# An output projection in seven half-size products, and both closing stages put into the list schedule

## The chip, the cores and the metric

The kernel runs on one core of one Trainium2 chip. The metric is the device time of one execution in microseconds (us), lower is better. The engines are TensorE (PE, matmuls into the accumulator memory PSUM), VectorE (DVE), ScalarE (ACT), GpSimd (POOL) and SyncE (SP, whose queue issues most DMA transfers).

## What is computed

One layer of an encoder for 1280 tokens of width D = 1024: a prompt of 1024 and a sample of 256 tokens, each with its own `gate` row. After a large input projection come a convolution branch and a bidirectional mLSTM branch. Cut to what matters here:

```python
g_conv, g_mlstm = jnp.split(jax.nn.sigmoid(gmerge), 2, axis=-1)
merged = g_conv * (y_conv @ w_proj_conv) + g_mlstm * (y_m @ w_proj_mlstm)
return x + gate * (merged @ w_out)            # then rms_norm(x, final_norm_g)
```

All three weight matrices here are 1024 x 1024, in float32.

## The kernel before

Every float32 product is made of three matmuls: each operand is split into a high part (a cast on ACT to the matmul's type) and a low part (the rest, a subtraction on DVE or POOL), and high x high, high x low and low x high are added up in PSUM. The input projection, up to about 1160 us, already multiplies by Strassen's scheme. The mLSTM stage and the convolution branch's projection follow until 1437 us. They are issued by a list scheduler, `Board`: each operation is recorded with its engine, an assumed duration, what it reads and writes and a step, and `board.play()` works out an order for each engine and issues the instructions in it. The two stages of this case come last. They are written by hand, in program order, behind that `play()`, and the framework adds the semaphores that their tiles need.

The tokens are worked on in two halves of 640 (five tiles of 128), the second half first. For each half:

- `merge` (L1799 and L1802 in the trace) calls `proj_y`, the product of y_m with w_proj_mlstm. The result has channels on the partitions: eight blocks of 128 channels, each with two accumulators of 320 tokens (q = 0, 1). For each accumulator PE runs 8 x 3 matmuls with 320 columns (L1596 to L1598). The weights are loaded in pairs of blocks (`raw`), and split by ACT (L275) and POOL (L276). `th` (the gate's part) and `zc` (the convolution branch's part, already multiplied) come from DRAM, through SP. DVE reads the accumulator in `times_1p` (L617), adds `zc` (L1799) and makes the low part `mL` (L1802); ACT makes the high part `mH`.
- `finish` is the output projection and the closing norm. Each half of w_out's columns is loaded and split by ACT (L1880) and DVE (L1881). For each of five token tiles and each half of the columns, `product_o` runs 8 x 3 matmuls with 512 columns (L1818 to L1820). In `residual`, DVE multiplies the accumulator by the gate (L1825) and adds it to `ob`, which holds x (L1826); ACT sums the squares (L1827), POOL multiplies by the final norm's weights (L1829). `norm_out` (from L1849) takes the root (ACT L1851), improves it with four small DVE instructions, scales the tile and sends it out. The very last column half of tile 4 is worked in two pieces of 256 columns (`last_part`, L1835 to L1840), and its scaling is shared by ACT (L1864) and DVE (L1865).

Every accumulator is a PSUM tile of its own, one bank with 512 floats in each partition. Eight of them are taken in turn:

```python
psD = [ctx.enter_context(tc.tile_pool(name=f"psD{n}", bufs=n, space=PSUM)) for n in (2, 6)]
def acc_d():
    taken[0] += 1
    return psD[(taken[0] - 1) % 8 < 6].tile([P, 512], F32, tag="acc", name="accd")
```

So PE can write one accumulator while DVE reads another, and it needs one again only eight accumulators later.

Of the kernel before, what the change touches and what calls it, by code (L numbers as in the profile page):

```python
# [9 lines left out]
F32 = mybir.dt.float32  # L10
# [171 lines left out]
def encoder_kernel(  # L182
# [40 lines left out]
    p1_dr = dram.tile([2, P, TH2], F32, name="p1_dr")  # L223

# [69 lines left out]
    hp = ctx.enter_context(tc.tile_pool(name="hp", bufs=1, side="right"))  # L294
# [1043 lines left out]
    thp = ctx.enter_context(tc.tile_pool(name="thp", bufs=3, side="right"))  # L1338
# [245 lines left out]
    def proj_y(src, y, acc_of, made=None):  # L1584

        for n2 in range(0, KT, 2):
            raws = made[0] if made and n2 == 0 else load_pair(wp, src, n2 * P, (n2 + 1) * P, 3)
            for nb in range(2):
                ws = made[1] if made and n2 + nb == 0 else [split_w(wp, r[:, :, nb * P:(nb + 1) * P], G) for r in raws]
                accs = [acc_of() for _ in range(2)]  # L1590
                for q in range(2):
                    qs = slice(q * TQ, (q + 1) * TQ)
                    for kt in range(KT):
                        wh, wl = (w[:, kt % 4, :] for w in ws[kt // 4])
                        yH, yL = (t[:, kt % 4, qs] for t in y[kt // 4])
                        PE.matmul(accs[q][:, :TQ], wh, yH, start=kt == 0, stop=False)  # L1596
                        PE.matmul(accs[q][:, :TQ], wh, yL, start=False, stop=False)  # L1597
                        PE.matmul(accs[q][:, :TQ], wl, yH, start=False, stop=kt == KT - 1)  # L1598
                    yield n2 + nb, q, accs[q]

# [153 lines left out]
    ym0.append(first_ym(1))  # L1754
    board.play()
    ym0 = [[[b.t for b in y] for y in ym0]]
    made_m = [b.t for b in raws_m], [[b.t for b in w] for w in ws_m]
    hand.close()
    mstack.close()
    bstack.close()  # L1760
    yr = ctx.enter_context(tc.tile_pool(name="yr", bufs=1, side="right"))

    def load_y(src, t0):
        v = src[:].rearrange("(k p) t -> p k t", p=P)
        res = []
        for n in range(2):
            yH, yL = (yq.tile([P, 4, TH2], F32R, tag=f"y{2 * n + part}", name="y") for part in range(2))
            for k in range(0, 4, 2):
                raw = yr.tile([P, 2, TH2], F32, tag="yraw", name="yraw")
                dma(raw[:], v[:, 4 * n + k:4 * n + k + 2, t0:t0 + TH2])  # L1770
                A.copy(yH[:, k:k + 2], raw[:])
                V.tensor_tensor(out=yL[:, k:k + 2], in0=raw[:], in1=fp(yH[:, k:k + 2]), op=ALU.subtract)
            res.append((yH, yL))
        return res

    psD = [ctx.enter_context(tc.tile_pool(name=f"psD{n}", bufs=n, space=PSUM)) for n in (2, 6)]
    taken = [0]
    wo_p = ctx.enter_context(tc.tile_pool(name="wo", bufs=2))  # L1780
    ep = ctx.enter_context(tc.tile_pool(name="ep", bufs=2))
    mgp = ctx.enter_context(tc.tile_pool(name="mgp", bufs=1))
    gbc = [mgp.tile([P, D], F32, name=f"gbc{s}") for s in range(2)]
    fng = mgp.tile([P, D], F32, name="fng")

    def acc_d():
        taken[0] += 1
        return psD[(taken[0] - 1) % 8 < 6].tile([P, 512], F32, tag="acc", name="accd")

    def merge(t0, y, mH, mL, made=None):  # L1790
        for n, q, acc in proj_y(wpm, y, acc_d, made):
            if q == 0:
                th = thp.tile([P, TH2], F32, tag="th", bufs=3, name="th")
                zc = ep.tile([P, TH2], F32, tag="zc", name="zc")
                dma(th[:], th_dr[D + n * P:D + (n + 1) * P, t0:t0 + TH2])
                dma(zc[:], zc_dr[n * P:(n + 1) * P, t0:t0 + TH2])
            qs = slice(q * TQ, (q + 1) * TQ)
            times_1p(th[:, qs], th[:, qs], acc[:, :TQ])
            V.tensor_tensor(out=th[:, qs], in0=th[:, qs], in1=zc[:, qs], op=ALU.add)  # L1799
            mh, ml = (m[n // 4][:, n % 4, qs] for m in (mH, mL))  # L1800
            A.copy(mh, th[:, qs])
            V.tensor_tensor(out=ml, in0=th[:, qs], in1=fp(mh), op=ALU.subtract)  # L1802

    def finish(c0, last, mH, mL):

        n5 = range(TH2 // P)
        ob = mgp.tile([P, 5, D], F32, tag="ob", name="ob")
        ssq = ep.tile([P, 5, 3], F32, tag="ssq", name="ssq")
        ms = ep.tile([P, 5], F32, tag="ms", name="ms")
        for j in n5:  # L1810
            dma(ob[:, j, :], x_rows(c0 + j))

        def product_o(pd, half, ws, j, cs=slice(0, 512)):
            ts_ = slice(j * P, (j + 1) * P)
            for k in range(4):
                kt = 4 * half + k
                sH, sL = mH[half][:, k, ts_], mL[half][:, k, ts_]
                PE.matmul(pd, sH, ws[0][:, k, cs], start=kt == 0, stop=False)  # L1818
                PE.matmul(pd, sH, ws[1][:, k, cs], start=False, stop=False)  # L1819
                PE.matmul(pd, sL, ws[0][:, k, cs], start=False, stop=kt == KT - 1)  # L1820

        def residual(pd, j, n2):
            ns = slice(n2 * 512, (n2 + 1) * 512)
            t = ep.tile([P, 4 * P], F32, tag="t", name="t")
            V.tensor_tensor(out=t[:], in0=pd, in1=gbc[0 if c0 + j < 8 else 1][:, ns], op=ALU.mult)  # L1825
            V.tensor_tensor(out=ob[:, j, ns], in0=ob[:, j, ns], in1=t[:], op=ALU.add)  # L1826
            A.activation(t[:], ob[:, j, ns], AF.Square, bias=zero[:, 0:1], scale=1.0,  # L1827
                         accum_out=ssq[:, j, n2:n2 + 1])
            G.tensor_tensor(out=ob[:, j, ns], in0=ob[:, j, ns], in1=fng[:, ns], op=ALU.mult)  # L1829

        def last_part(pd, i):

            ns = slice(512 + 256 * i, 768 + 256 * i)
            t = ep.tile([P, 4 * P], F32, tag="t", name="t")[:, 0:256]
            V.tensor_tensor(out=t, in0=pd[:, 0:256], in1=gbc[0][:, ns], op=ALU.mult)  # L1835
            V.tensor_tensor(out=ob[:, 4, ns], in0=ob[:, 4, ns], in1=t, op=ALU.add)
            V.tensor_tensor_reduce(out=t, in0=ob[:, 4, ns], in1=ob[:, 4, ns], op0=ALU.mult, op1=ALU.add, scale=1.0,
                                   scalar=0.0, accum_out=ssq[:, 4, 1 + i:2 + i])
            if i == 0:
                V.scalar_tensor_tensor(out=ms[:, 4:5], in0=ssq[:, 4, 1:2], scalar=1.0 / D, in1=ms[:, 4:5], op0=ALU.mult,  # L1840
                                       op1=ALU.add)

        def part_sums():
            V.tensor_scalar(out=ms[:], in0=ssq[:, :, 0], scalar1=1.0 / D, scalar2=EPS, op0=ALU.mult, op1=ALU.add)

        def norm_out(j0, j1):
            n, js = j1 - j0, slice(j0, j1)
            v, r, t = ms[:, js], *(ep.tile([P, n], F32, tag=f"n{i}", name=f"n{i}")[:] for i in range(2))
            V.scalar_tensor_tensor(out=v, in0=ssq[:, js, 2 if last and j0 == 4 else 1], scalar=1.0 / D, in1=v, op0=ALU.mult,  # L1849
                                   op1=ALU.add)  # L1850
            A.activation(r, v, AF.Sqrt, bias=zero[:, 0:1], scale=1.0)  # L1851
            V.reciprocal(r, r)
            if n == 1:
                V.scalar_tensor_tensor(out=t, in0=r, scalar=r, in1=v, op0=ALU.mult, op1=ALU.mult)
            else:
                V.tensor_tensor(out=t, in0=r, in1=r, op=ALU.mult)
                V.tensor_tensor(out=t, in0=t, in1=v, op=ALU.mult)
            V.tensor_scalar(out=t, in0=t, scalar1=-0.5, scalar2=1.5, op0=ALU.mult, op1=ALU.add)
            V.tensor_tensor(out=r, in0=t, in1=r, op=ALU.mult)
            for j in range(j0, j1):  # L1860
                rj = r[:, j - j0:j - j0 + 1]
                if last and j == 4:
                    hs = slice(0, D // 2), slice(D // 2, D)
                    A.activation(ob[:, j, hs[0]], ob[:, j, hs[0]], AF.Copy, bias=0.0, scale=rj)  # L1864
                    V.scalar_tensor_tensor(out=ob[:, j, hs[1]], in0=ob[:, j, hs[1]], scalar=rj, in1=fng[:, hs[1]],  # L1865
# [7 lines left out]
        def weights_o(n2, half):  # L1873
# [8 lines left out]
            return wh, wl  # L1882

        for n2 in range(2):
            ws = [weights_o(n2, half) for half in range(2)]
            if last and n2 == 1:

                for j in range(4):
# [64 lines left out]
```

## Time and profile before

| what | value |
|---|---|
| runs of the kernel | 1671.61, 1673.78, 1674.88 us |
| median | 1673.78 us |
| profiled execution | 1672.24 us |
| its span in the trace | 1670.5 us |
| mean granted clock of PE | 0.992 |
| first matmul of the merge | at 1437.19 us |
| first matmul of the last output projection | at 1605.22 us |

The page gives each engine's busy time as a share of the span, and follows back the chain of work that ended last. Rows of groups give the busy time and the mean duration of one instruction, and behind the last bar the idle time ahead of them with what ended it. Rows of the timeline give the start and the duration in us. Consecutive matmuls overlap, so the distance of their starts, not their duration, is what one costs.

### The profile page before, as it was taken

What the parts mean: (1) busy time and instruction counts of PE and PEld (TensorE: products, weight loads), DVE (VectorE), ACT (ScalarE), POOL (GpSimd) and SP (SyncE); (2) the same over time, 40 slices, a digit from 0 to 9 for tenths busy, and PEclk for the clock granted to TensorE, in tenths of its full rate; (3) what the DMA queues carried; (4) which work ended last, traced back from release to release, by engine and by line L of the source; (5) the groups of instructions that cost most, each with busy time, mean ns of one, the idle gap of its engine ahead of it and who ended that gap; (6) DMA issues with size and microseconds to landing.
All of it is one profiled execution on the core that took longest, in us unless ns stands there. A gap on an engine that the chain in (4) does not pass through costs nothing.

```text
span 1670.5 us, 27720 instructions
## 1 busy us (share of the span) xinstructions
PE 1634.5 (98%) x10552; PEld 1566.6 (94%) x10552; DVE 993.8 (59%) x1698; ACT 573.4 (34%) x1113; POOL 677.1 (41%) x498
## 2 busy tenths in 40 slices
PE   6999999999999999999999999999999999999997
PEld 3989999999999999999999999999888898998986
DVE  4885334556555566556656886652157777555645
ACT  4643332134453222222222211121256665333322
POOL 2243333335564666677666643333210001323412
PEclk8999999999999999999999999999999999999999
DMA  9434335324553122221222555458888855773631
GB/s 361 127 97 142 102 106 117 79 71 125 144 156 104 51 70 70 83 82 59 59 75 71 142 132 143 124 132 256 284 250 274 274 188 176 254 265 108 242 109 64
DMA packets 284697, 240.83 MB, mean 144 GB/s; under 512 B 96164, under 2 KB 239764, under 8 KB 284564
## 3 DMA queue, kind: packets, MB, share of 16 engines
q1 hardware_dynamic: 284388, 238.78, 46.7%
q8 instruction: 84, 1.38, 0.3%
q14 instruction: 49, 0.40, 0.1%
q10 hardware_dynamic: 176, 0.27, 0.0%
HBM read 170.12 MB, written 68.89 MB: 143 GB/s over the span
## 4 chain that ended last, share of the span: by engine, by line
PE 94%; DVE 2%; DMA 2%; SPq 1%; ACT 1%; issue 0%; POOL 0%; DVEq 0%; ACTq 0%
PE acc L807 64%; PE u L1441 3%; PE qc L1401 3%; PE accd L1597 2%; PE accd L1596 2%; PE accd L1598 2%; PE accd L1820 2%; PE accd L1818 2%; PE accd L1819 2%; PE acc L1665 2%; PE acc L1666 2%; PE acc L1667 2%; PE misc L1524 1%; PE misc L1484 1%; PE misc L436 1%; DMA raw<-in_w_in_dram 1%
## 5 line engine op out<-in xcount | busy, mean ns | idle before, releaser
L318 POOL TENSOR_TENSOR wl<-comb,wh 128x512 fp32r<-128x512 f32 x176 | 248.9, 1415 | 289.9 <-ACT wh L317 279.0
L716 DVE TENSOR_TENSOR q<-acc,q 128x640 f32<-128x640 f32 x272 | 220.8, 819 | 222.1 <-PE acc L807 216.8
L318 POOL TENSOR_TENSOR wl<-raw,wh 128x512 fp32r<-128x512 f32 x138 | 191.6, 1389 | 232.2 <-ACT wh L317 220.2
L807 PE MATMUL acc<-xt,wh 128*128 128x320 f32 x1408 | 264.0, 309 | 0.0
L807 PEld LDWEIGHTS acc<-xt,wh 128*128 128x128 f32 x1408 | 220.8, 188 | 0.2
L317 ACT CAST wh<-comb 128x512 fp32r<-128x512 f32 x176 | 108.8, 619 | 298.0 <-PE acc L807 261.3
L317 ACT CAST wh<-raw 128x512 fp32r<-128x512 f32 x138 | 85.3, 619 | 273.4 <-PE acc L807 204.1
L807 PE MATMUL acc<-xt,wl 128*128 128x320 f32 x704 | 160.5, 309 | 0.0
L1624 POOL TENSOR_TENSOR wl<-raw,wh 128x512 fp32r<-128x512 f32 x28 | 36.5, 1309 | 222.9 <-ACT wh L1623 222.4
L807 PEld LDWEIGHTS acc<-xt,wl 128*128 128x128 f32 x704 | 117.7, 188 | 0.0
L672 DVE TENSOR_TENSOR comb<-raw 128x512 f32<-128x512 f32 x88 | 71.4, 811 | 44.6 <-DMA raw<-in_w_in_dram 32.4
L875 POOL TENSOR_TENSOR big<-big,q 128x640 f32<-128x640 f32 x48 | 78.6, 1638 | 37.1 <-DVE q L716 28.7
L614 ACT ACTIVATE q<-q,zero 128x640 f32<-128x640 f32 x76 | 63.0, 831 | 82.6 <-DVE q L716 78.4
L672 DVE TENSOR_TENSOR comb<-raw,comb 128x512 f32<-128x512 f32 x44 | 46.7, 1061 | 63.3 <-POOL wl L318 63.2
L807 PE MATMUL acc<-t3L,wh 128*128 128x320 f32 x352 | 81.5, 313 | 2.7 <-DVE t3L L369 2.7
L807 PE MATMUL acc<-t3H,wh 128*128 128x320 f32 x352 | 81.3, 313 | 1.4 <-ACT t3H L368 1.4
L807 PE MATMUL acc<-b00H,wh 128*128 128x320 f32 x352 | 82.5, 316 | 0.0
L807 PE MATMUL acc<-b10H,wh 128*128 128x320 f32 x352 | 80.7, 311 | 0.8 <-ACT q L730 0.8
L807 PE MATMUL acc<-t3H,wl 128*128 128x320 f32 x352 | 81.4, 313 | 0.0
L807 PE MATMUL acc<-b11H,wh 128*128 128x320 f32 x352 | 81.3, 312 | 0.0
L807 PE MATMUL acc<-b00L,wh 128*128 128x320 f32 x352 | 80.8, 311 | 0.0
L807 PE MATMUL acc<-b00H,wl 128*128 128x320 f32 x352 | 80.5, 310 | 0.0
(322 smaller groups left out, 4116.4 us busy)
## 6 DMA issues: line engine op xcount, KB each, us to landing
raw<-in_w_in_dram SPq DMA_DIRECT2D x120, 256.0 KB
raw<-in_w_in_dram SPq DMA_DIRECT2D x34, 512.0 KB
th<-th_dr SPq DMA_DIRECT2D x31, 320.0 KB
th_dr<-q SPq DMA_DIRECT2D x28, 320.0 KB
raw<-in_w_proj_conv_dram SPq DMA_DIRECT2D x16, 512.0 KB
raw<-in_w_proj_mlstm_dram SPq DMA_DIRECT2D x16, 512.0 KB
raw<-in_w_out_dram SPq DMA_DIRECT2D x16, 512.0 KB
k<-kn_dr SPq DMA_DIRECT2D x56, 128.0 KB
```

Source lines behind the costliest of these rows:

```text
L317: op("ACT", .63, lambda: A.copy(wh[:], src()), r=r, w=[wh])
L318: op("POOL", 1.4, lambda: G.tensor_tensor(out=wl[:], in0=src(), in1=fp(wh[:]), op=ALU.subtract), r=[*r, wh], w=[wl])
L614: A.activation(out, in_, AF.Tanh, bias=zero[:, 0:1], scale=0.5)
L672: op("DVE", .9, lambda: V.tensor_tensor(out=t[:], in0=x(), in1=y(), op=o), r=[x.tok, y.tok], w=[t])
L716: op("DVE", .82, lambda: V.tensor_tensor(out=two(dst()), in0=acc[:, :, 0:TQ], in1=two(t()), op=ALU.add), r=[acc, t.tok], w=[dst.tok])
L807: PE.matmul(acc[:, q, 0:TQ], st_[:, k_, :], m_[:, q * TQ:(q + 1) * TQ], start=k_ == 0 and n == 0, stop=k_ == 3 and n == 2)
L875: op("POOL", 1.65, lambda: G.tensor_tensor(out=dst(), in0=dst(), in1=t(), op=ALU.mult), r=[dst.tok, t.tok], w=[dst.tok])
L1401: PE.matmul(pq[:, 0:HD + 2], qTs[i][:, kd, c * P:(c + 1) * P], C[:, kd, :], start=kd == 0, stop=kd == 1)
L1441: PE.matmul(pu[:, db, 0:HD + 2], k[:, db * P:(db + 1) * P], wv[:], start=True, stop=True)
L1596: PE.matmul(accs[q][:, :TQ], wh, yH, start=kt == 0, stop=False)
L1597: PE.matmul(accs[q][:, :TQ], wh, yL, start=False, stop=False)
L1624: op("POOL", 1.36, lambda wh=wh, wl=wl, src=src: G.tensor_tensor(out=wl[:], in0=src(), in1=fp(wh[:]), op=ALU.subtract), r=[raw, wh], w=[wl])
```

## The change

The two closing stages become parts of the list schedule, and the output projection is multiplied by Strassen's scheme on pairs of token tiles.

- The merge of all 16 blocks (both halves) is recorded on the board (`merge`, L1855 to L1857 for the matmuls, L619 and L1863 on DVE). It leaves the merged values unsplit in SBUF (`mg`). Its PSUM tiles now have two banks, `[P, 2, 512]`, three in one pool and one in another; the accumulators of q = 0 and q = 1 are the halves of one tile.
- Beside the merge, `prepare(k)` loads w_out in quarter tiles and makes the seven factors of the scheme: B11, B21 and T2 stay in SBUF, t1, t3, t4 and b22 are stored to DRAM in split form and fetched later (`fetch`, 2 MB each). Splits are L1776 (ACT) and L1778 (DVE), combinations L1800 (DVE). `second_ym` (L1822) loads and splits the other half's y_m there too.
- Then the output projection runs on three groups of token tiles: quad0 (5, 6 with 8, 9), quad1 (0, 1 with 2, 3) and a pair (7 with 4). A quad's operand is cut into four quarters (two tiles by half of the channels); `sums` and `rest` (L1921) combine them on DVE or POOL, `splits` split them (L1776, L1778), and `product` multiplies seven times: for each tile 4 x 3 matmuls of 512 columns (L1947 to L1949). ACT copies the first product out of PSUM (`copy_out`, L1961). DVE adds the others (`plus`, L1974), multiplies by the gate and adds x (`gated`, L1988 and L1992, once on POOL); ACT sums the squares (L1997). `norm` (L2017 to L2040) scales the rows, `weigh` (POOL, L2122) multiplies some by the final norm's weights ahead of that. In the last tile, 4, the last product is worked in two pieces of 256 columns (L2230 to L2237); its root, and after it that of tile 7, follow (L2241 to L2249).

The core of the diff:

```diff
-    hand.close()
...
+    psD, psO = (ctx.enter_context(tc.tile_pool(name=nm, bufs=n, space=PSUM)) for nm, n in (("psD", 1), ("psO", 3)))
...
+    def bank():
+        k = len(banks)
+        if k % 2 == 0:
+            banks.append(buf(*((psO, [P, 2, 512], F32, "acc", 3) if k % 8 < 6 else (psD, [P, 2, 512], F32, "acc", 1))))
+        else:
+            banks.append(banks[-1])
+        b = banks[-1]
+        return (lambda: b[:, k % 2]), (b, k % 2)
...
+    def prepare(k):
...
+        def away(nm, x, spent=True):
+            h = buf(pr, [P, 512], F32R, "pr", 7)
+            l = x if spent else buf(pr, [P, 512], F32R, "pr", 7)
+            split_into(lambda: h[:], lambda: l[:].bitcast(F32R), lambda: x[:], [x], h, l)
+            for i, t in enumerate((h, l)):
+                op("SP", 256, lambda i=i, t=t: dma(late_dr[nm][i, :, k], fp(t[:])), r=[t], w=[(nm, i, k)], low=True)
...
+        kept_split(B11, r11)
+        kept_split(B21, r21)
+        away("b22", r22, False)
+        comb(r22, r22, r12)
+        comb(r12, r12, r11)
+        comb(r11, r22, r11, ALU.add)
+        away("t1", r12)
+        away("t3", r22)
+        kept_split(T2, r11)
+        comb(r21, r21, r11)
+        away("t4", r21)
...
+        for q in range(2):
+            acc, tok = bank()
...
+            for part in range(4):
+                ops = [*ws[part // 2], *((t, k % 4) for t in y[part // 2] for k in range(2 * part, 2 * part + 2))]
+                op("PE", .88, lambda part=part, mm=mm: mm(part), r=ops + ([tok] if part else []), w=[tok])
+            op("DVE", .48, lambda acc=acc, qs=qs: times_1p(th[:, qs], th[:, qs], acc()[:, :TQ]), r=[tok, (th, q)], w=[(th, q)])
+            op("DVE", .49, lambda qs=qs: V.tensor_tensor(out=mg[:, n % 4, qs], in0=th[:, qs], in1=zc[:, qs], op=ALU.add),
+               r=[(th, q), (zc, q)], w=[(mg, p) for p in at_q(q)])
...
+        def banks(self, pool):
+            b = buf(pool, [P, 2, 512], F32, "acc", 1 if pool is psD else 3)
+            return [((lambda j=j: b[:, j]), (b, j)) for j in range(2)][:self.n]
...
+        def copy_out(self, dst, tag):
+
+            t = o_tile(tag)
+            for j in range(self.n):
+                ap, tok = dst[j]
+                op("ACT", .57, lambda j=j, ap=ap: A.copy(t[:, j * 512:(j + 1) * 512], ap()), r=[tok], w=[(t, j)])
+            return t
...
+    for st, nxt in ((quad0, quad1), (quad1, pair)):
+        st.scratch()
+        b = st.banks(psO)
+        do(st, "a11", B11, b)
+        s1 = st.copy_out(b, "raw")
+        parts(st, "a12")
+        st.rest()
+        parts(st, "s2")
+        a = st.banks(psO)
+        do(st, "a12", B21, a)
+        parts(st, "s3")
+        c = st.banks(psO)
+        do(st, "s2", T2, c)
+        u2 = st.plus(s1, c, o_tile("o"))
+        st.plus(s1, a)
+        st.gated(0, 0, s1)
+        if st is quad1:
+            weigh(0, 0)
...
+        g = st.banks(psO)
+        do(st, "s4", b22, g)
+        if st is quad0:
+            t3 = fetch("t3")
+        st.norm(1)
+        st.plus(u2, g)
+        st.gated(0, 1, u2)
+        if st is quad1:
+            weigh(0, 1)
+        st.norm(0)
```

The order of the instructions on the engines, at the two places that matter most. The first is the merge. On PE, this stands in a block of the changed kernel (the ninth; `acc_15761` is its two-bank tile, `b00` and `b10` are y_m's halves by channel, H and L their high and low parts), where the accumulator q = 0 ends and q = 1 begins:

```order
L1857 MATMUL acc_15761<-b10H_15372,wl_15696 128x320
L1855 MATMUL acc_15761<-b00H_15209,wh_15662 128x320
L1856 MATMUL acc_15761<-b00L_15220,wh_15662 128x320
L1857 MATMUL acc_15761<-b00H_15209,wl_15673 128x320
L1855 MATMUL acc_15761<-b00H_15209,wh_15662 128x320
L1856 MATMUL acc_15761<-b00L_15220,wh_15662 128x320
L1857 MATMUL acc_15761<-b00H_15209,wl_15673 128x320
L1855 MATMUL acc_15761<-b00H_15209,wh_15662 128x320 [waits DVE_49]
L1856 MATMUL acc_15761<-b00L_15220,wh_15662 128x320
```

and on DVE, for the same block, with the last rows of the block ahead of it:

```order
L619 SCALAR_TENSOR_TENSOR th_15584<-th_15584,acc_15677 128x320 [waits PE_49]
L1863 TENSOR_TENSOR mg1_15562<-th_15584,zc_15619 128x320 [waits DVE_49]
L619 SCALAR_TENSOR_TENSOR th_15628<-th_15628,acc_15761 128x320 [waits DMAHW0_49,PE_49]
L1863 TENSOR_TENSOR y0_15808<-th_15628,zc_15736 128x320 [waits DMAHW7_49,DVE_49]
L619 SCALAR_TENSOR_TENSOR th_15628<-th_15628,acc_15761 128x320 [waits PE_49]
L1863 TENSOR_TENSOR y0_15808<-th_15628,zc_15736 128x320 [waits DVE_49]
```

The first L619 on `acc_15761` waits on PE for the L1857 just ahead of the waiting L1855, and that L1855 waits on DVE for this L619. Before, at the change from one accumulator to the next (`accd_15465` and `accd_15466`, two tiles), stood on PE:

```order
L1598 MATMUL accd_15465<-y2_14941,wl_15462 128x320
L1596 MATMUL accd_15466<-y0_14439,wh_15457 128x320 [waits DVE_49]
L1597 MATMUL accd_15466<-y1_14527,wh_15457 128x320
L1598 MATMUL accd_15466<-y0_14439,wl_15458 128x320
L1596 MATMUL accd_15466<-y0_14439,wh_15457 128x320
```

and on DVE:

```order
L617 SCALAR_TENSOR_TENSOR th_15491<-th_15491,accd_15465 128x320 [waits DMAHW5_49,PE_49]
L1799 TENSOR_TENSOR th_15491<-th_15491,zc_15492 128x320 [waits DMAHW2_49,DVE_49]
L1802 TENSOR_TENSOR mL_15106<-th_15491,mH_15104 128x320 [waits Activation_49]
L617 SCALAR_TENSOR_TENSOR th_15491<-th_15491,accd_15466 128x320 [waits PE_49]
L1799 TENSOR_TENSOR th_15491<-th_15491,zc_15492 128x320 [waits DVE_49]
```

PE's wait there was for the reading of a bank eight accumulators earlier. Now it is for the reading of the accumulator that PE has just finished, and it stands six matmuls into the next one. It stands so in nine of the 16 blocks; in the others DVE's first reading is ordered behind the whole of q = 1.

The second place is DVE in the output stage. After the change, behind the third product of quad0 (`o`, `raw`: scratch tiles; `y2`, `y3`: the rows of x; `late`-fetched factors are PE's operands):

```order
L1974 TENSOR_TENSOR o_16522<-acc_16485,raw_16436 128x1024 [waits DMAHW3_49,DMAHW4_49,DMAHW2_49,DMAHW5_49,DMAHW1_49,DMAHW6_49,DMAHW0_49,PE_49]
L1778 TENSOR_TENSOR wl_16531<-raw_16111,wh_16524 128x512 [waits Activation_49]
L1974 TENSOR_TENSOR raw_16436<-acc_16451,raw_16436 128x1024 [waits DVE_49]
L1988 TENSOR_TENSOR raw_16436<-raw_16436,y2_15882 128x1024 [waits DVE_49]
L1778 TENSOR_TENSOR wl_16558<-mg1_15562,wh_16547 128x512 [waits PE_49,Activation_49]
L1992 TENSOR_TENSOR y2_15882<-y2_15882,raw_16436 128x1024 [waits DVE_49]
L1974 TENSOR_TENSOR raw_16574<-acc_16518,o_16522 128x1024 [waits PE_49]
L1778 TENSOR_TENSOR wl_16587<-mg1_15562,wh_16571 128x512 [waits Activation_49]
L1778 TENSOR_TENSOR wl_16600<-mg1_15562,wh_16595 128x512 [waits PE_49,Activation_49]
L1974 TENSOR_TENSOR o_16614<-acc_16565,raw_16574 128x1024 [waits DVE_49,PE_49]
```

Before, in the output stage of a half:

```order
L1825 TENSOR_TENSOR t_16792<-accd_16667,gbc0_15097 128x512 [waits PE_49]
L1826 TENSOR_TENSOR ob_16639<-ob_16639,t_16792 128x512 [waits DVE_49]
L1825 TENSOR_TENSOR t_16797<-accd_16668,gbc0_15097 128x512 [waits PE_49]
L1826 TENSOR_TENSOR ob_16639<-ob_16639,t_16797 128x512 [waits DVE_49]
L1825 TENSOR_TENSOR t_16802<-accd_16669,gbc0_15097 128x512 [waits PE_49,Activation_49]
L1826 TENSOR_TENSOR ob_16639<-ob_16639,t_16802 128x512 [waits DVE_49]
```

Where DVE had two instructions of 512 elements for each accumulator of 24 matmuls, it now has sums, gates and splits of 512 and 1024 for each product of 24 matmuls, and each next product on PE needs a split that stands in this queue.

546 lines of the change are left out of this document (385 added, 161 removed).

## Prediction

> **What bounds the kernel now.** I read the page first, then the waits of TensorE, then rows of the timeline at the end.
>
> ```profile
> PE 1634.5 (98%) x10552; PEld 1566.6 (94%) x10552; DVE 993.8 (59%) x1698; ACT 573.4 (34%) x1113; POOL 677.1 (41%) x498
> PE 94%; DVE 2%; DMA 2%; SPq 1%; ACT 1%; issue 0%; POOL 0%; DVEq 0%; ACTq 0%
> PE accd L1819 <- DVE wl L1881: 1.8, 1, 1.8
> 1610.00:1670.50 60.50, 50.77 (x244) 42.18 (x242) 30.03 (x54) 12.84 (x26) 11.64 (x9) 0.96 0.14 53
> ```
>
> The chain that ended last is 94% TensorE (PE). The third line is one row of PE's waits from 1380 us on (total, times, longest): the only one there over 0.4 us whose waiter is in the two stages that change. The last is a window: its length, then PE, weight loads, DVE, ACT, POOL busy, granted clock, DMA share, GB/s. DVE is half busy. So the end is PE's matmuls, laid end to end, and a short tail behind them.
>
> ```profile
> L1597 PE MATMUL accd<-y,wh 128*128 128x320 f32 x256 | 79.4, 310 | 0.0
> 1437.19 0.31 PE L1596 MATMUL accd<-y,wh 128*128 128x320 f32 x1
> 1483.73 0.31 PE L1597 MATMUL accd<-y,wh 128*128 128x320 f32 x1
> 1491.97 0.31 PE L1596 MATMUL accd<-y,wh 128*128 128x320 f32 x1
> 1629.72 0.39 PE L1820 MATMUL accd<-wh,mL 128*128 128x512 f32 x1
> 1635.22 0.39 PE L1820 MATMUL accd<-wh,mL 128*128 128x512 f32 x1
> ```
>
> From the fourth line to the third, 56 matmuls of 320 columns lie in 8.24 us: 0.147 us each (0.31 is the length of one, they overlap). From the fifth to the sixth, 24 of 512 columns in 5.50 us: 0.229 each. The merge has 3 x 256 = 768 of the former, 112.9 us; put together, it would reach from 1437.2 to 1550.1. The span ends at 1670.5, so the output stage costs 120.4 us now, tail included.
>
> **The change, term by term.** The merge keeps its 768 matmuls. The output projection had the work of 10 tiles x 2 halves x 8 x 3 = 480 matmuls of 512 columns; two quads of 7 x 2 x 4 x 3 = 168 and a pair of 84 make 420. Sixty fewer at 0.229 are **13.7 us**, and the 1.8 us wait on L1881 has no successor: at most 15.5 us to gain.
>
> **Merge: new waits.** A PSUM tile is now two banks, and the two accumulators of a block (q0, q1) are its halves. The order rows above show what follows: DVE's reading of q0 stands behind the first six matmuls of q1, and the rest of q1 waits for DVE. That stands in 9 of the 16 blocks. What one costs:
>
> ```profile
> 1636.36 0.39 PE L1818 MATMUL accd<-wh,mH 128*128 128x512 f32 x1
> 1638.59 0.50 PE L1819 MATMUL accd<-wl,mH 128*128 128x512 f32 x1 [1.84 <-DVE wl L1881]
> 1638.93 0.39 PE L1820 MATMUL accd<-wh,mL 128*128 128x512 f32 x1
> 1656.57 0.39 PE L1820 MATMUL accd<-wh,mL 128*128 128x512 f32 x1
> 1657.00 0.69 DVE L1825 TENSOR_TENSOR t<-accd,gbc 128x512 f32<-128x512 f32 x1 [3.83 <-PE accd L1820]
> L617 DVE SCALAR_TENSOR_TENSOR th<-th,accd 128x320 f32<-128x320 f32 x32 | 15.3, 482 | 18.1 <-PE accd L1598 10.2 <-DMA th<-th_dr 6.8 <-DMA raw<-in_w_proj_mlstm_dram 1.0
> ```
>
> The matmul's overlap is lost (0.31 - 0.147 = 0.16); DVE starts 0.04 behind PE's end (1656.96 to 1657.00), and I take the same back; the read takes 0.48; the first matmul behind a wait is 0.11 longer (0.50 for 0.39). That is 0.83 if DVE is free, 7.5 us for nine. DVE is not always: a split or sum of 0.7 to 1.2 us that has begun must end first, and DVE will be some 60% busy. Half of one of these in about half the blocks brings it to 1.05, **9.5 us**; a whole one each time to 1.6, 14.4. All of it is on the path, since no other matmul is ahead of the waiting one on PE. Not below 7.5, unless the waits are met early, a rival below.
>
> The Trainium skill ("PSUM — Partial Sum Buffer", Summary: rules for kernel authors) says to read PSUM in another bank than the running matmul's. Here q0 and q1 do lie in different banks, so the rule would have no wait and the merge no loss; the row of before with L1825 agrees in that PE goes on beside such reads. The wait comes from the tile, not from the bank.
>
> Also in the merge: sixteen quarter tiles of w_out, 44 DVE instructions on 512 elements for splits and factors (in place of L1881's 16 of twice the size), 8.4 MB of stores. Their cover is PE, for 113 us.
>
> **Output stage: DVE.** DVE had two instructions per product; now it has sums of products, splits of each factor and gates. PE's first three products of the first quad are 72 x 0.229 = 16.5 us. The copy by ACT between its two halves (L1961) blocks the second half as above: 0.16 + 0.04 + 0.57 + 0.04 + 0.11 = 0.9. From 17.4 us on, I count what the order has left on DVE. Prices:
>
> ```profile
> 1512.77 1.22 DVE L1881 TENSOR_TENSOR wl<-raw,wh 128x1024 fp32r<-128x1024 f32 x1
> 1513.90 0.68 DVE L1825 TENSOR_TENSOR t<-accd,gbc 128x512 f32<-128x512 f32 x1
> 1514.62 0.69 DVE L1826 TENSOR_TENSOR ob<-ob,t 128x512 f32<-128x512 f32 x1
> L1865 DVE SCALAR_TENSOR_TENSOR ob<-ob,n,fng 128x512 f32<-128x512 f32 x1 | 0.8, 753 | 0.0
> 1664.62 0.16 DVE L1849 SCALAR_TENSOR_TENSOR ms<-ssq,ms 128x1 f32<-128x1 f32 x1
> L1835 DVE TENSOR_TENSOR t<-accd,gbc 128x256 f32<-128x256 f32 x2 | 0.8, 410 | 0.0
> ```
>
> A successor that needs nothing starts 0.08 before its forerunner's end (1513.90, not 1513.99), one that needs it 0.03 after. So: 32 instructions of 1024 at 1.15 = 36.8; 28 splits and sums of 512 at 0.61 = 17.1; 13 of the pair, mixed, at 0.66 = 8.6; 12 scalings (L2040) at 0.67 = 8.0; 28 small ones at 0.18 = 5.0; eight of 256 at 0.42 = 3.4. Together **78.9 us**, beside 348 x 0.229 = 79.7 of PE: two engines equally full, each needing the other's results in turn. Three more terms:
>
> - DVE runs dry where it needs a product that PE began late. A product of the pair is 12 matmuls, 2.75 us; two such give **5**, one 3, a little more 7.
> - POOL gets ten instructions of 512 or more there (sums for the next tokens, L2122, two gates). How they stand beside DVE:
>
> ```profile
> L1826 DVE TENSOR_TENSOR ob<-ob,t x19: 691/786/1841, 1514.6 to 1657.7; 128x512 f32<-128x512 f32 x19
> L1826 DVE TENSOR_TENSOR ob<-ob,t 128x512 f32<-128x512 f32 x19 | 18.5, 972 | 0.7
> 1522.67 1.84 DVE L1826 TENSOR_TENSOR ob<-ob,t 128x512 f32<-128x512 f32 x1
> L1829 POOL TENSOR_TENSOR ob<-ob,fng x19: 1283/1295/1899, 1517.8 to 1659.4; 128x512 f32<-128x512 f32 x19
> ```
>
> The sum L1826 takes 0.69 alone and 1.84 where POOL's L1829 (1.3 us) began with it; its mean is 0.97. So 0.28 per POOL instruction now, 1.15 where they meet. DVE will be fuller: I take 0.6, **6 us**; ends 2.8 and 11.5.
> - The tail. From L1849 to the end are 5.7 us now. Behind it come another tile's root, its small steps (0.75) and two scalings on ACT of 0.72: +2.2, **8.0** (L1864 below).
>
> Output stage: 17.4 + 78.9 + 5 + 6 + 8.0 = 115.3, for 120.4: -5.1. Ends 110.1 and 122.8.
>
> ```profile
> 1666.04 0.72 ACT L1864 ACTIVATE ob<-ob,n 128x512 f32<-128x512 f32 x1 [0.93 <-DVE n L1859]
> span 1670.5 us, 27720 instructions
> ```
>
> **Sum.** +9.5 - 5.1 = +4.4. The profiled execution took 1672.24 us, 1.74 beside its span, so 1676.6; the median of the runs shown, 1673.78, is 1.5 above it: **1678.2 us**. By the terms' ends: 7.5 - 10.3 = -2.8 (1671) and 14.4 + 2.4 = +16.8 (1690.6).
>
> **Rivals.**
>
> PE keeps the lead, faster: if DVE's queue stays ahead of PE, the output stage is PE's 96.2 + 3 x 0.9 + the tail of before 7.9 (1662.6 to 1670.5) + 2.2 = 109.0, so -11.4, with the merge at its floor of 7.5: -3.9, **1669.9**. For it: the two loads are equal within 1 us, and DVE's first operands are made in the merge. Against: it asks that neither ever waits for the other, and in the pair two halves of a tile wait for DVE's sums (L1974) besides. It decides where DVE's idle and blocked time falls under 5 us; were the nine waits met early too, 1662.4.
>
> Little contention: POOL at 0.28 each (2.8), idle 4, merge 8.3: 111.1 - 120.4 + 8.3 = -1.0, **1672.8**, no change. For it the mean of 0.97 above; against it, DVE's fuller queue.
>
> POOL always meets DVE: ten times 1.15, 11.5 instead of 6: **1683.7**. The row of 1.84 is for it, the median of 0.786 against. The Trainium skill ("SBUF — State Buffer", SBUF: two separate sides) calls the port pair of the two an exclusive lock held for a whole instruction; the 1.84 agrees, and the rule by itself speaks for this case.
>
> Late transfers:
>
> ```profile
> 1430.00:1490.00 60.00, 60.00 (x410) 59.78 (x409) 31.43 (x52) 20.34 (x36) 21.25 (x15) 1.00 0.78 273
> 1445.00:1450.00 5.00, 5.00 (x36) 5.00 (x35) 2.73 (x7) 0.86 (x2) 0.00 (x0) 1.00 1.00 362
> ```
>
> The merge must move 10.5 MB of th and zc, 7.3 of weights, 2.6 of y, 4.2 of w_out, 2.6 of x and gates and 8.4 of stores: 35.6 MB, at 362 GB/s 98 us and hidden, at 273 GB/s 130 us. SP's queue is in order and the loads of zc wait on it for DVE, those of raw weights for POOL's splits. At 273 the merge is 17 us longer, which swallows the other waits: 17 - 5.1 = +11.9, **1685.7**. Against it: 362 has been reached.
>
> **Chances.** Forecast (1673 to 1684) 0.42, PE in the lead 0.18, little contention 0.18, POOL always 0.11, late transfers 0.11. What a measurement tells from no change is some 0.2%, 3.3 us: faster ends at 1670.4, slower begins at 1677.1. Faster: 0.15 of PE in the lead and 0.03 of little contention, 0.18. Same: 0.14, 0.03, and 0.10 of the forecast, 0.27. Slower: 0.55. The range 1667 to 1688 leaves out the deepest gains and the latest transfers.
>
> **What would show it.** In PE's waits, nine on L619 of some 0.8 to 1 us of idle and three on L1961; if they are missing, the merge term falls. PE's busy share after the merge under 90%, with waits on DVE's splits L1778; near 100%, and PE leads. DVE instructions of 1024 elements over 1.3 us beside POOL's L2122 or L1921 show contention. Waits on th, zc, raw or late factors show transfers. I am wrong if DVE is idle over 15 us in the output stage, or if one merge wait is well under 0.8.

## The result and the profile after

The changed kernel takes 1685.55 us (median of 4 runs, 1684.89 to 1686.32), the kernel before 1673.58 in the runs beside it: 12.0 us more, a ratio of 1.0073 with a 95% interval of 1.0055 to 1.009. The profiled execution took 1685.18 us, its span 1683.1, 12.6 above that of before. From the page of the changed kernel, the engines' busy time and the chain that ended last:

```profile
PE 1626.4 (97%) x10480; PEld 1555.1 (92%) x10480; DVE 1050.0 (62%) x1764; ACT 588.1 (35%) x1145; POOL 678.2 (40%) x492
PE 86%; DVE 5%; DMA 5%; issue 1%; SPq 1%; ACT 1%; POOL 0%; ACTq 0%; DVEq 0%; POOLq 0%
```

TensorE's share of the chain falls from 94 to 86%, and those of DVE and DMA rise from 2% each to 5%. Its waits in the two stages, where there had been one (total, times, longest):

```profile
PE acc L1855 <- DVE th L619: 8.9, 9, 3.5
PE acc L1947 <- DVE raw L1974: 2.3, 1, 2.3
PE acc L1947 <- ACT raw L1961: 2.0, 3, 0.7
PE acc L1947 <- DVE o L1974: 0.8, 1, 0.8
```

Four windows of the changed kernel, in the columns that the prediction explains: the merge, the two quads, from the pair's first matmul to the end, and the tail behind the last matmul. Below them the tail of the kernel before:

```profile
1437.30:1563.80 126.50, 117.60 (x770) 115.23 (x769) 84.78 (x122) 42.75 (x71) 43.60 (x30) 0.97 0.86 286
1563.90:1644.10 80.20, 78.85 (x337) 62.81 (x337) 69.37 (x84) 28.84 (x58) 12.86 (x6) 1.00 0.73 248
1644.10:1683.10 39.00, 20.60 (x97) 16.06 (x95) 32.00 (x62) 13.99 (x30) 10.65 (x7) 0.86 0.46 164
1668.40:1683.10 14.70, 0.01 (x1) 0.00 (x0) 8.82 (x25) 3.42 (x7) 2.23 (x2) 0.63 0.22 72
```

```profile
1662.60:1670.50 7.90, 0.01 (x1) 0.00 (x0) 3.52 (x12) 1.02 (x2) 0.00 (x0) 0.70 0.51 200
```

The merge takes 126.5 us for the same 768 matmuls that filled 112.9: 13.6 us lost. The output stage takes 119.2 (80.2 and 39.0) instead of 120.4: 1.2 gained. Together they are 12.4 of the span's 12.6 us; the merge begins 0.1 us later, and the rest is rounding. In the last 39 us PE is busy for half of the time and DVE for 32.

In the merge, eight of the nine waits look like the first two matmuls below, and one like the others (timeline of PE):

```profile
1506.24 0.31 PE L1857 MATMUL acc<-b00H,wl 128*128 128x320 f32 x1
1507.13 0.41 PE L1855 MATMUL acc<-b00H,wh 128*128 128x320 f32 x1 [0.58 <-DVE th L619]
1478.67 0.31 PE L1857 MATMUL acc<-y,wl 128*128 128x320 f32 x1
1482.52 0.64 PE L1855 MATMUL acc<-y,wh 128*128 128x320 f32 x1 [3.54 <-DVE th L619]
1482.96 0.47 PE L1856 MATMUL acc<-y,wh 128*128 128x320 f32 x1
1483.22 0.47 PE L1857 MATMUL acc<-y,wl 128*128 128x320 f32 x1
```

The first wait makes 0.89 us from start to start where 0.147 is usual, and the next step 0.10 longer: 0.84 us. Six cost that, two a little more (1.1 and 1.3), 7.5 in all. The long one costs 3.7. Behind it the matmuls lie 0.26 to 0.27 us apart, for about 5 us more, another 2.5: the granted clock is at half. Seven of the nine stand six matmuls into q1, as in the order rows; the long one and the next but one stand 18 into it. What DVE did meanwhile, and two windows of the same kernel, one around the wait and one behind it:

```profile
1478.94 0.88 DVE L619 SCALAR_TENSOR_TENSOR th<-th,acc 128x320 f32<-128x320 f32 x2 [1.36 <-DMA th<-th_dr]
1481.16 0.89 DVE L1863 TENSOR_TENSOR mg<-th,zc 128x320 f32<-128x320 f32 x2 [1.34 <-DMA zc<-zc_dr]
1481.98 0.49 DVE L619 SCALAR_TENSOR_TENSOR th<-th,acc 128x320 f32<-128x320 f32 x1
1477.60:1482.90 5.30, 1.75 (x11) 1.49 (x10) 2.23 (x6) 1.14 (x2) 2.49 (x2) 0.83 0.96 322
1481.80:1488.50 6.70, 5.98 (x24) 5.98 (x25) 4.45 (x7) 2.18 (x4) 1.28 (x1) 0.54 1.04 367
```

DVE was a whole block behind: it still had to read the block ahead of this one, and stood waiting for its th and then its zc, with the DMA engines nearly full (share 0.96, 322 GB/s during the wait). With accumulators in tiles of their own PE does not notice, as the first run below shows.

### The profile page after: what moved, and what is told of

Same layout as the page of the kernel before. It is cut to its first block, busy times and chain, and to the rows that moved or that the text cites. A ratio compares the mean times of both kernels' runs of the same rounds, so it can differ in the third digit from the quotient of the medians.

```text
span 1683.1 us, 27858 instructions
## 1 busy us (share of the span) xinstructions
PE 1626.4 (97%) x10480; PEld 1555.1 (92%) x10480; DVE 1050.0 (62%) x1764; ACT 588.1 (35%) x1145; POOL 678.2 (40%) x492
## 4 chain that ended last, share of the span: by engine, by line
PE 86%; DVE 5%; DMA 5%; issue 1%; SPq 1%; ACT 1%; POOL 0%; ACTq 0%; DVEq 0%; POOLq 0%
PE acc L809 64%; PE u L1443 3%; PE qc L1403 3%; PE acc L1650 2%; PE acc L1651 2%; PE acc L1652 2%; PE acc L1947 2%; PE acc L1948 2%; PE acc L1949 2%; DMA th<-th_dr 1%; PE misc L1526 1%; PE misc L1486 1%; SPq L308 1%; DMA raw<-in_w_proj_mlstm_dram 1%; DMA raw<-in_w_in_dram 1%
## 5 line engine op out<-in xcount | busy, mean ns | idle before, releaser
L320 POOL TENSOR_TENSOR wl<-raw,wh 128x512 fp32r<-128x512 f32 x168 | 236.4, 1409 | 306.3 <-ACT wh L319 279.9
L319 ACT CAST wh<-raw 128x512 fp32r<-128x512 f32 x168 | 103.6, 620 | 323.4 <-PE acc L809 210.4
L1609 POOL TENSOR_TENSOR wl<-raw,wh 128x512 fp32r<-128x512 f32 x28 | 36.6, 1310 | 223.3 <-ACT wh L1608 216.2
L809 PE MATMUL acc<-t3H,wh 128*128 128x320 f32 x352 | 81.2, 312 | 1.4 <-ACT t3H L370 1.4
L809 PE MATMUL acc<-b00H,wh 128*128 128x320 f32 x352 | 82.4, 316 | 0.0
L809 PE MATMUL acc<-t2L,wh 128*128 128x320 f32 x352 | 80.4, 310 | 0.1
```

Source lines behind the costliest of these rows:

```text
L319: op("ACT", .63, lambda: A.copy(wh[:], src()), r=r, w=[wh])
L320: op("POOL", 1.4, lambda: G.tensor_tensor(out=wl[:], in0=src(), in1=fp(wh[:]), op=ALU.subtract), r=[*r, wh], w=[wl])
L809: PE.matmul(acc[:, q, 0:TQ], st_[:, k_, :], m_[:, q * TQ:(q + 1) * TQ], start=k_ == 0 and n == 0, stop=k_ == 3 and n == 2)
L1609: op("POOL", 1.36, lambda wh=wh, wl=wl, src=src: G.tensor_tensor(out=wl[:], in0=src(), in1=fp(wh[:]), op=ALU.subtract), r=[raw, wh], w=[wl])
```

## The experiments

Each profiled execution reaches the merge at another time (1436.5 to 1441.2 us, by what came before it), so I compare the length of each stage, from its own first matmul on. All stages are worked out from the timeline of PE as above. "Gap" is the time from the merge's last matmul to the output stage's first. Each stage's length is that of one profiled execution. The list scheduler orders everything anew after each edit, so the order of DVE's instructions changes a little in places that the edit does not touch.

| kernel | median us | ratio to before, 95% | merge | gap | quads | pair to end | of it tail |
|---|---|---|---|---|---|---|---|
| changed | 1685.55 | 1.0073 (1.0055 to 1.009) | 126.5 | 0 | 80.3 | 38.9 | 14.7 |
| single banks | 1683.59 | 1.0057 (1.0042 to 1.0072) | 113.3 | 5.9 | 82.8 | 38.9 | 14.6 |
| y later | 1686.18 | 1.0078 (1.0063 to 1.0093) | 125.2 | 0 | 80.3 | 38.7 | 13.0 |
| POOL to DVE | 1686.21 | 1.0074 (1.0057 to 1.009) | 122.7 | 0 | 80.3 | 41.0 | 18.2 |
| both edits | 1685.18 | 1.0066 (1.0051 to 1.0081) | 114.2 | 5.9 | 82.4 | 41.0 | 18.2 |
| one read | 1673.08 | 0.9995 (0.9984 to 1.0007) | 112.8 | 0 | 80.6 | 38.7 | 12.9 |
| one copy | 1672.00 | 0.9989 (0.9979 to 0.9999) | 112.8 | 0 | 79.4 | 38.7 | 12.9 |
| tail | 1673.13 | 0.9994 (0.9983 to 1.0005) | 113.9 | 0 | 80.4 | 39.4 | 17.6 |
| no scale | 1668.89 | 0.997 (0.9959 to 0.998) | 112.8 | 0 | 81.2 | 35.3 | 10.9 |
| plain pair | 1664.41 | 0.9941 (0.9927 to 0.9954) | 112.8 | 0 | 79.8 | 30.1 | 7.4 |
| no weigh | 1666.30 | 0.9943 (0.993 to 0.9955) | 112.8 | 0 | 81.2 | 30.2 | 7.4 |
| quad0 unscaled | 1673.57 | 0.9993 (0.9984 to 1.0002) | 112.8 | 0 | 80.6 | 38.9 | 14.7 |

**Single banks.** A tile of its own for each accumulator:

```diff
...
-        return (lambda: b[:, k % 2]), (b, k % 2)
+        b = buf(psG, [P, 512], F32, "acc", 8)
+        return (lambda: b[:]), b
...
+    gstack.close()
+    psD, psO = (ctx.enter_context(tc.tile_pool(name=nm, bufs=n, space=PSUM)) for nm, n in (("psD", 1), ("psO", 3)))
```

> Each accumulator of the merge is a one-bank tile of its own again (eight in turn), everything else as in the changed kernel. Theory A (the half-tile wait): the nine PE waits on L619 go, the merge falls from 126.7 us to 113 to 114 (112.9 of matmuls), the clock stays at 1.0 there, and the time falls by some 13 us, to about 1672.5. Theory B (late transfers): th and zc still come late with DMA engines full around 1470 to 1490 us, PE waits for something else in their place, and at most the eight short waits (7.5 us) are gained: about 1678.

The merge fell to 113.3 us, as theory A says, with one wait of 0.6 left, at its start. DVE still stood for th and zc at the same place, 3.2 us in all, and PE did not (timeline of DVE):

```profile
1481.01 0.88 DVE L619 SCALAR_TENSOR_TENSOR th<-th,acc 128x320 f32<-128x320 f32 x2 [1.81 <-DMA th<-th_dr]
1483.30 1.44 DVE L1859 TENSOR_TENSOR mg<-th,zc 128x320 f32<-128x320 f32 x2 [1.41 <-DMA zc<-zc_dr]
```

But the time fell by 2 us only. From the timeline of PE and a window of this kernel:

```profile
1554.28 0.31 PE L1853 MATMUL acc<-b10H,wl 128*128 128x320 f32 x1
1560.28 0.77 PE L1943 MATMUL acc<-b,wh 128*128 128x512 f32 x1 [5.69 <-issue]
1559.40:1566.20 6.80, 5.92 (x15) 4.75 (x16) 6.73 (x6) 0.62 (x1) 5.27 (x2) 0.54 0.59 204
```

Between the stages PE stood still for 5.7 us, waiting for nothing that the profile shows, and then ran at half clock: 5.9 us of gap and 2.5 in the quads. The edit had added a change of PSUM pools at this place; that it is the cause is argued from the place and from the next round, where it is gone. Another 3.9 us are the later start of the merge in this execution; what made it later was not followed up. So the run shows in the merge's length what the half tiles cost, and the gap and the start hide it in the time.

**y later.** The loading of the other half's y_m moved by three blocks, the preparation by three, three, one and one:

```diff
-        if i < 6 and i % 2 == 0 and i < 4:
-            ym1.append(second_ym(i // 2))
-        if i in (4, 6, 9, 11):
-            prepare((4, 6, 9, 11).index(i))
+        if i in (3, 5):
+            ym1.append(second_ym((3, 5).index(i)))
+        if i in (7, 9, 10, 12):
+            prepare((7, 9, 10, 12).index(i))
```

> The two-bank tiles stay, but the loading and splitting of the other half's y_m and the preparation of the weight factors begin three blocks later, so that th comes in time. Theory A: nine short PE waits of 0.6 to 1.1 us stay, the 3.5 us one and the 6.8 us of half clock behind it go: 6 us gained, about 1679.5. Theory B (the long wait comes from full DMA engines whatever the order): a wait of over 2 us turns up elsewhere in the merge, within 2 us of the changed kernel's 1685.5.

```profile
PE acc L1855 <- DVE th L619: 9.4, 11, 2.8
1446.58 0.41 PE L1855 MATMUL acc<-y,wh 128*128 128x320 f32 x1 [2.79 <-DVE th L619]
1446.04 0.49 DVE L619 SCALAR_TENSOR_TENSOR th<-th,acc 128x320 f32<-128x320 f32 x1 [4.54 <-DMA raw<-in_w_proj_mlstm_dram]
```

The 3.5 us wait is gone, but there are now eleven waits, and one of 2.8 us in the first block; the merge takes 125.2. Nothing gained beyond the measurement, as theory B has it. Ahead of the reading that PE waited for, DVE had stood 4.5 us for a transfer, by the profile a load of weights. That full DMA engines were behind it is not shown; what is shown is that a late reading by DVE lands on PE while the half tiles stand.

**POOL to DVE.** The late POOL instructions on DVE:

```diff
-            op("POOL", 1.5, lambda j=j: G.tensor_tensor(
+            op("DVE", .69, lambda j=j: V.tensor_tensor(
...
-        nxt.sums(True)
+        nxt.sums(st is quad0)
...
-    st.gated(0, 1, u4, square=False, pool=True)
+    st.gated(0, 1, u4, square=False)
```

> The eleven POOL instructions of the output stage behind 1600 us (products with the final norm's weights, two of the pair's gate, the pair's sums) are run by DVE, the fuller engine. Theory A (a POOL instruction holds DVE up for its whole length): DVE gets 7 us of work more and loses 10.9 us of being held up: 3 to 5 us faster, about 1681.5. Theory B (DVE's own load is what counts, the long durations come from something else): 5 to 7 us slower, about 1691.

Neither came: the time did not change (1686.21 for 1685.55). By stages, the output stage became 2.1 us longer (121.3 for 119.2); the merge was 3.8 us shorter, its long wait 2.4 us without half clock, but began 3.5 later, and neither of these two is shown to come from the edit. In the changed kernel DVE and POOL meet like this (timeline):

```profile
1656.29 3.48 DVE L2040 SCALAR_TENSOR_TENSOR mg<-mg,q,fng 128x512 f32<-128x512 f32 x2
1655.85 1.67 POOL L1988 TENSOR_TENSOR raw<-raw,y 128x512 f32<-128x512 f32 x1 [3.20 <-DVE raw L1974]
1657.60 1.62 POOL L1992 TENSOR_TENSOR y<-y,raw 128x512 f32<-128x512 f32 x1
1660.30 1.40 DVE L2040 SCALAR_TENSOR_TENSOR mg<-mg,q,fng 128x512 f32<-128x512 f32 x2
1673.44 1.26 POOL L2122 TENSOR_TENSOR y<-y,fng 128x512 f32<-128x512 f32 x1 [4.07 <-ACT o L1997]
1673.60 1.39 DVE L2234 CUSTOM_DVE_ANT_0 raw<-y 128x256 f32<-128x256 f32 x1
```

Two scalings take 3.48 us beside POOL and 1.40 without. In this way eleven DVE instructions from 1604 us on lose 10.8 us, each against its length without POOL, and with the instructions on DVE none of these losses is left. The holding up is real, and so was its size. But DVE had 7 us more to do in exchange, and stood 5 us longer (9.1 us idle behind quad0's third product, for 3.9, added up from DVE's timeline), some 3 of them for PE's products and 2 for ACT. At the end it made the tail longer, from 14.7 to 18.2.

**Both edits** together:

> The edits of the two runs single bank and POOL to DVE together. If they are independent, as theory A has it (one in the merge, one in the output stage), the gains add up: about 1668.5, some 5 us below the kernel before the change. If the output stage was only catching up on DVE work that the merge left over, or transfers set the end, less than either sum: 1672 or more.

The time, 1685.18, is in the second range, but the stages show another reason than the one given for it: the merge at 114.2, the gap at the pool change, the longer tail, as in the two runs. It adds nothing to tell the theories apart.

**One read.** The half-tile wait taken away without a change of pools: DVE reads a whole block at once.

```diff
-            op("DVE", .48, lambda acc=acc, qs=qs: times_1p(th[:, qs], th[:, qs], acc()[:, :TQ]), r=[tok, (th, q)], w=[(th, q)])
...
+        whole = tok[0]
+        op("DVE", .81, lambda: times_1p(two(th[:]), two(th[:]), whole[:, :, :TQ]),
+           r=[(whole, 0), (whole, 1), (th, 0), (th, 1)], w=[(th, 0), (th, 1)])
...
```

> The two-bank tiles stay, and so do the PSUM pools, but DVE reads both halves of a merge block in one instruction of 640 elements, behind the whole block (and adds zc in one). No PE wait stands in the middle of a tile, and no pool is changed between the stages, which is what took 5.7 us of PE and 6.8 us of half clock in the run with single banks. Theory A: the merge takes 113 to 114 us as there, the output stage follows at once and takes its 119: 13 us less than the changed kernel, about 1672.5, level with the kernel before. Theory B (what the merge gains is given back by a later stage that cannot begin sooner, as transfers of the late factors): a wait on DMA in the output stage and 1678 or more.

```profile
1437.20:1550.00 112.80, 112.80 (x770) 112.80 (x769) 75.21 (x86) 41.90 (x71) 45.39 (x30) 1.00 0.92 316
```

Theory A: the merge is matmul behind matmul at full clock again, 13.7 us shorter, and the time falls by 12.5 us to 1673.08, level with the kernel before. The transfers (316 GB/s now) did not stop it, though DVE still stood 3.2 us for th.

**One copy.** In the quads, ACT copies the first product out of both halves at once:

```diff
+            if self.n == 2:
+                ap, toks = self.both(dst)
+                op("ACT", 1.0, lambda: A.copy(self.tile(t), ap()), r=toks, w=[(t, 0), (t, 1)])
+                return t
```

> The run before, and in the quads ACT copies the first product in one instruction of 1024 elements, behind both its halves. The two PE waits on L1961 in the quads (0.95 us each) go. If PE sets the pace of the quads: 1.5 to 2 us less than the run before. If DVE does: no difference.

Both waits went, and one of 0.7 us for DVE's split came in, so the quads became only 1.2 us shorter (80.6 to 79.4). The quads follow PE's waits, which speaks for PE setting their pace. The whole is 1.1 us less, which the intervals of the two runs do not separate.

**Tail.** The run before with the POOL instructions on DVE, and `board.step = step[0] + 1` for `+ 4` in `norm`:

> The run before, with the late POOL instructions on DVE as in the run POOL to DVE, and the closing norm of a quad ordered three steps sooner, so that the time in which DVE waits for the pair's products (3 to 5 us there) has scalings to do. Theory A (what was lost in that run is DVE idle time, what is bound at the end is DVE's queue behind the last product): the tail behind the last matmul falls from 14.7 us to 11 to 13, and the whole is 2 to 4 us below the run before, 1667 to 1669. Theory B (the sum of DVE's work decides, and POOL takes some off): 2 us above it, as in the first trial.

A miss for theory A: the tail went up to 17.6 us, from 12.9 in the run before. The whole went up by 1.1 us, which the intervals do not separate.

**No scale.** The twelve scalings of the quads' rows left out, on the run with one read:

> The run with one read, and the twelve scalings L2040 of the two quads' rows are left out (their rows go out unscaled): 8 us of DVE's work. If DVE's queue sets the end of the output stage: 6 to 8 us less than the run with one read, the tail near 8 us. If PE does up to its last matmul and only the pair's own work stands behind it: 3 us or less.

8 us of DVE's work less gave 4.2 us in the medians and 2.8 in the output stage (from 119.3 to 116.5), all of it behind the pair's first matmul: 38.7 to 35.3. In the medians it fell between the two theories, and which of the twelve mattered was open.

**quad0 unscaled.** Only the eight scalings of quad0 left out:

> The run with one read, and only the eight scalings of quad0's rows are left out (its rows go out unscaled; quad1's four stay). With all twelve left out the profiled span fell by 1.9 us and the output stage by 2.8. Theory A (DVE sets the pace only in the last 39 us): these eight, 5.4 us of DVE's work in the middle of the quads, bring 0 to 0.5 us. Theory B (DVE's queue is full throughout): they bring two thirds of what all twelve did, 2 us or more.

1673.57 beside 1673.08: nothing, as theory A says. 5.4 us of DVE's work in the middle of the stage, where DVE is busy for 69 of 80 us, are worth nothing; by the difference of the two runs, the four scalings of quad1, which fall into the last stretch, are worth about 3 us.

**Plain pair.** Tiles 7 and 4 in the ordinary way, on top of one read and one copy. The core:

```diff
+    def straight(r, half, dst, cs=slice(0, 512)):
...
+        for kh in range(2):
+            rhs = ((B11, b12), (B21, b22))[kh][half]
+            wh, wl = st.ws[r, kh][0]
...
+    straight(0, 0, acc[0])
+    st.gated(0, 0, o_tile("o"), acc[0])
...
+    st.splits((1, 0), st.places[1, 0])
+    st.splits((1, 1), st.places[1, 1])
+    straight(0, 1, acc[1])
+    st.gated(0, 1, o_tile("o"), acc[1])
+    straight(1, 1, acc[2])
+    st.gated(1, 1, o_tile("o"), acc[2])
     weigh(1, 1)
+    st.norm(0)
```

> The run with one read and one copy, and the last two token tiles (7 and 4) are multiplied in the ordinary way, tile by tile: 96 instead of 84 matmuls of 512 columns on PE, but no sums of operands or products, four splits instead of seven, every accumulator in a tile of its own, tile 7 finished ahead of tile 4. In the merge one more quarter of w_out is split and stored. Theory A (the quads run at PE's pace, and the Strassen product's gain is given back in the last 39 us, where DVE has too much to do for 19 us of matmuls): the stretch from the first matmul of the pair to the end falls from 38.7 us to 22 of matmuls plus a tail of 8 to 10, 30 to 32; the whole is 7 to 9 us below the run with one copy, about 1664, 0.55% below the kernel before. Theory B (DVE's queue is full from the first quad on, so its backlog is only met elsewhere): 3 us or less, 1669 or more.

The stretch from the pair to the end, in the kernel with one copy and in this one:

```profile
1631.60:1670.30 38.70, 21.98 (x97) 17.09 (x95) 32.70 (x62) 14.17 (x30) 10.46 (x7) 0.83 0.45 155
```

```profile
1631.90:1662.00 30.10, 22.68 (x121) 19.18 (x119) 21.01 (x53) 9.22 (x22) 4.51 (x3) 0.92 0.31 105
```

Theory A: with 12 matmuls more, DVE is busy for 21.0 us instead of 32.7, the tail is 7.4 instead of 12.9, and the stretch is 8.6 us shorter. PE has no wait over 0.1 us left in the pair. The whole takes 1664.41 us: 7.6 below one copy, 21 below the changed kernel, and a ratio of 0.9941 (0.9927 to 0.9954) to the kernel before. It beats both. The edit changes three things at once: no extra sums and fewer splits, tiles that are not shared, and tile 7 finished ahead of tile 4, so that its root (2.2 us of the tail) no longer stands at the end. How the 8.6 us divide among them was not tried.

**No weigh.** Without quad1's POOL instructions, on top of it:

> The run before, and quad1's halves are no longer multiplied by the final norm's weights on POOL (four instructions); its rows are scaled and weighted in one DVE instruction each, as quad0's. If POOL's four instructions cost DVE more in waiting (3.6 us there) than they save (four of 0.67): 0.5 to 1 us faster; if DVE is no longer what sets the end: no difference.

0.9943 beside 0.9941: no difference in the ratios. The medians lie 1.9 us apart, and in the profiled executions the quads are 1.4 us longer, with three waits of PE for DVE's splits (L1778) of 0.3 to 0.9 us in place of one of 0.7; the stretch that the question is about, from the pair on, is 30.1 and 30.2. So POOL's four instructions no longer count there, as the missing waits of PE have it.

## Why the prediction was right or wrong

The direction was right, and 1685.55 lies in the range; the forecast of +4.4 us was less than half of the +12.0. By the stages, 4.1 us of what is missing lie in the merge (13.6 for 9.5) and 3.9 in the output stage (119.2 for 115.3).

- **The gain on PE** was put at 13.7 us for sixty matmuls. Shown: 11.9. The new products' matmuls lie 0.2333 us apart (5.60 us for 24), not 0.229, so 420 take 98.0.
- **The merge's waits** were put at 9.5 us for nine, 0.83 each if DVE is free. The mechanism, the number and that price were right: eight cost 7.5 us, most of them 0.84. (Of that 0.58 is idle time; the sign that I gave, 0.8 to 1 us of idle, mixed up idle time and cost.) The term that was mis-sized is the ninth: 6.2 us. I had priced DVE's being busy, not its waiting for th and zc, and left that wait in a rival (late transfers) as if it were spread over the whole merge. It struck one block, 3.7 us, and brought the half clock, 2.5, which no part of the prediction has. The upper end, 14.4, held it.
- **DVE held up by POOL** was put at 6 us between 2.8 and 11.5. It was 10.8, from eleven POOL instructions where I had counted ten: nearly the rival in which they always meet. The POOL to DVE run shows the holding up and also that ending it gives nothing, since DVE must then do the work.
- **The output stage** was put at 115.3 by a sum of DVE's work, idle time and holding up from the first quad on; measured 119.2. That this sum comes out near the measured length with 10.8 in place of 6 does not make it right: idle, busy and held-up time always fill the stretch. The step that failed is "two engines equally full". In the quads PE sets the pace (one copy gains there, quad0's scalings don't), and the waits on the splits L1778 that I gave as a sign are missing in the changed kernel. DVE sets it from the pair on, where 39.0 us hold 19.6 us of matmuls. There PE's waits on L1974 and the tail of 14.7 us give back the gain: 6.8 us more tail than before, of which 3.6 are DVE's queue when the last matmul ends (the last piece is read 4.3 us behind it, before 0.6), 1.0 a meeting with POOL and 2.2 the other tile's root. The 2.2 was predicted. The sign of being wrong came true too: in the 119.2 us DVE is busy for 101.4, so idle for 17.8, over the 15 that I had named; 10.8 of them lie in the quads, and 5.2 behind its last instruction.
- **Late transfers** as a rival of its own (the merge at 130 us) did not come; the one-read run moves its data in 112.8 us.
- **The two rules that I had cited.** By the Trainium skill ("PSUM — Partial Sum Buffer", Summary: rules for kernel authors) the halves' different banks need no wait; the single-banks run agrees, where the tiles differ as well as the banks: the nine waits went but for one of 0.6 us, so they came from the tile. The exclusive lock of the Trainium skill ("SBUF — State Buffer", SBUF: two separate sides) agrees with the 10.8 us, better than my 6.

In sum: 13.6 us lost in the merge by how accumulators share a tile; 11.9 gained by fewer matmuls, of which 4.3 went back in PE's waits (6.4 for 2.1 before) and 6.8 in the tail. That leaves 0.8 of the 1.2 that the output stage became shorter; the last 0.4 I did not trace.

## What to carry to other kernels

Look at which accumulators share a tile, not only at which share a bank: where a reader of one half stands between the matmuls of the other, PE can wait once per tile, and a late operand of that reader becomes PE's. Fewer matmuls are worth their time only where PE sets the pace, so ask it for each stretch: here Strassen's scheme paid in the quads (the last kernels keep it there and are below the kernel before), and in the last pair the ordinary product was 8.6 us shorter with 12 matmuls more, since nothing comes behind to cover DVE's work. Work taken off an engine is a test of that: 5.4 us in one stretch brought nothing and 2.7 in another brought about 3.

## What was not expected of the hardware

- **Half clock behind a wait.** Behind PE's waits of 3.54 us (changed kernel) and 5.69 us (single banks) the granted clock was at half for about 6.8 us, which cost 2.5 us more in each. Behind 2.79 us (y later) and 2.37 us (POOL to DVE) it was not. Behind 2.25 us on L1974's sum it was in three kernels (y later, one read, one copy) and not in three others (changed, single banks, quad0 unscaled). A window of the kernel with one read, behind that wait:

```profile
1651.50:1654.90 3.40, 3.40 (x16) 3.03 (x15) 3.33 (x5) 1.89 (x5) 2.16 (x2) 0.59 0.73 247
```

  The Trainium skill ("TensorE: Matmul & The Clock Gate", Part 1: The HAM clock gate) has the clock halved after an idle window of about 3.4 us, with windows that run freely. Lengths of 3.4 and 6.8 us and the different outcome of the same wait agree with that; that a wait of 2.25 us was enough, shorter than its window, does not follow from it.

  These six kernels are also a test of the last stretch. With the half clock PE's last matmul ends 1.4 to 1.5 us later after the pair's first, but the whole stretch takes 38.7 us instead of 38.9. So what delays PE there does not reach the end, as it must be where DVE sets the pace; and the tails of 12.9 or 13.0 us for 14.7 in the table are no gain, only a later last matmul.
- **Spacing of matmuls.** The same shape, 128x512, came every 0.2290 us in the output stage before and every 0.2333 after (also in the plain pair's kernel), 1.8 us over 420. What makes the 4 ns was not tried, and stays open.
- **Small instructions are held up too.** A sum and a scaling of two numbers per partition (L2017, L2018), 0.15 and 0.17 us alone, took 1.25 and 1.22 us beside POOL's L2122 (timeline of the changed kernel):

```profile
1650.17 1.25 DVE L2017 TENSOR_TENSOR v<-ssq 128x2 f32<-128x2 f32 x1
1651.45 1.22 DVE L2018 TENSOR_SCALAR v<-v 128x2 f32<-128x2 f32 x1
1652.59 0.15 DVE L2017 TENSOR_TENSOR v<-ssq 128x2 f32<-128x2 f32 x1
1649.72 2.93 POOL L2122 TENSOR_TENSOR mg<-mg,fng 128x512 f32<-128x512 f32 x2 [17.77 <-ACT o L1997]
```
